# Eight of the 22 gate and up feature tiles of a ConvGLU formed from quarter blocks by seven products in place of eight

## The chip, the cores and the metric

The kernel runs on one core of a Trainium2 chip. The metric is the device time of one execution in microseconds (us). The median of three runs of the kernel before is 916.2 us, the lowest 915.85 and the highest 916.44 us. One further execution was recorded by the hardware profiler: it took 916.33 us, of which 914.6 us are the span from the first to the last instruction of the program, so 1.7 us lie around the span.

## The reference

One encoder layer over 512 tokens of width 1024, all in float32: a layer norm, a mixer of two attention head groups, a cross-attention to 256 memory tokens, and a gated feed-forward block, each followed by a residual sum and a layer norm. The change concerns the last block only. Cut to it, with 2816 features:

```python
def conv_glu(h, w_gate, w_up, conv_w, conv_b, w_down):
    g = h @ w_gate                      # (512, 1024) @ (1024, 2816)
    g = conv of width 3 along the tokens, per feature, plus conv_b
    return (gelu(g) * (h @ w_up)) @ w_down
```

## The kernel before, in words

**Arithmetic.** [...] To keep accuracy, every operand is split into a rounded part `hi` and the rest `lo`, and each product is made of three matmuls: hi·hi, hi·lo and lo·hi. The split takes one copy on ScalarE (ACT, line 134) and one subtraction on VectorE (DVE, line 136); the function is `split`, line 132.

**The gate and up stage.** The normed activations `h` lie transposed on chip in `h2T`, a pair (hi, lo), 8 blocks of 128 model rows by 512 tokens. `to_T` (line 202) makes them for 128 tokens at a time: eight transposes on TensorE into PSUM, then the split out of PSUM (lines 211 and 212). The 2816 features are 22 tiles of 128 (`NF`). For each tile f, `w_cols` (line 142) loads 1024 x 128 of `w_gate` and of `w_up` over SyncE's (SP's) DMA queue into a `raw` buffer and splits it. `gemm_fm` (line 168) then runs 8 x 3 matmuls with the weight block stationary and 512 tokens moving, once for gate (PSUM tag `g`) and once for up (PSUM tag `s`). The tail of the tile (lines 1356 to 1365) makes the convolution with one activation on ACT (Identity with scale and bias) and two scalar_tensor_tensor on DVE that read the gate sum in PSUM, then Gelu on ACT, then the product with up on DVE, written to `act[:, f, :]`.

**The first two tiles.** While the last 256 tokens are not yet normed and transposed, the gate and up of tiles 0 and 1 are begun on the first 256 tokens: `pre_gemm(i, 0)` runs 24 matmuls with 256 moving columns, and `pre_gemm(i, 1)` runs the other 256 columns later (lines 1328 to 1343). They use the PSUM tags `t`, `o` and both buffers of `g`.

**The stage behind.** The down product (from line 1394) takes the 22 tiles of `act` one after the other: it splits each into buffers of the tag `x`, splits 128 rows of `w_down`, and runs 24 matmuls of 512 columns for each.

**What sets the order.** Each engine runs its own queue in order. Within `manual_schedule` the order of TensorE is the order of the program text; everywhere else, and for ACT and DVE throughout the feed-forward block, a planner orders the instructions when the program is built. The loop over f in the kernel before is outside such a block, so there the planner orders TensorE too. Buffers are rotated by tags, and an instruction that takes a buffer waits until its last reader is done: `raw` has 3 buffers, `hi` and `lo` have 6 each (three feature tiles ahead), `gb` 2, `c` 3 (the convolution), `x` 12. PSUM has two buffers of `g` (one bank each), two of `s` (two banks each), one `t` and one `o`.

Of the kernel before, what the change touches and what calls it, by code (L numbers as in the profile page):

```python
# [9 lines left out]
F32 = mybir.dt.float32  # L10
F32R = mybir.dt.float32r
I32 = mybir.dt.int32
AF = mybir.ActivationFunctionType
ALU = mybir.AluOpType
# [3 lines left out]
P = 128  # L18
D = 1024
S = 512  # L20
NB = S // P
KD = D // P
# [3 lines left out]
NF = DFF // P  # L26
# [22 lines left out]
]  # L49

MEM_AT = (2, 0)
WARM = (12, 3)
CI, CF, CS, CMA, CM1, CM3 = 0, 128, 129, 130, 514, 770
CW = 898
# [17 lines left out]
def hymba_layer(ctx: ExitStack, tc: tile.TileContext, A, cst_d, out):  # L72
    nc = tc.nc
    X = mybir.AxisListType.X

    def pool(name, bufs=1, side="left", space=None):
        kw = {} if space is None else {"space": space}
        if space is None:
            kw["side"] = side
        return tc.tile_pool(name=name, bufs=bufs, **kw)  # L80

    cpool = ctx.enter_context(pool("const", side="right"))
    wpool = ctx.enter_context(pool("weights", side="right"))
    spool = ctx.enter_context(pool("small", bufs=3, side="right"))
    xpool = ctx.enter_context(pool("x2k", side="right"))
    spool.tile([P, 32], F32, tag="sfill", bufs=1, name="sfill")
    dpool = ctx.enter_context(tc.tile_pool(name="scratch", bufs=1, space=DRAM))

    cst = cpool.tile([P, CW], F32, name="cst")
    ident = cst[:, CI : CI + P]  # L90
    mhalf = cpool.tile([P, 1], F32, name="mhalf")
# [47 lines left out]
    def wsplit(raw, shape, eng=None):  # L139
        return split(raw, shape, wpool, "hi", 6, wpool, "lo", 6, eng)  # L140

    def w_cols(w, c0, eng=None):
        raw = wpool.tile([P, KD, P], F32, tag="raw", bufs=3, name="raw")
        nc.sync.dma_start(raw, w.rearrange("(k p) f -> p k f", p=P)[:, :, c0 : c0 + P])
        return wsplit(raw, [P, KD, P], eng)
# [10 lines left out]
    def on_pe(ins):  # L156
        if pe["pin"]:
            pe["pin"] = False
            tc.keep_in_program_order(ins)

    def pin():

        pe["pin"] = True

    def mm(o, l, r, first, last):
        on_pe(nc.tensor.matmul(o, l, r, start=first, stop=last))  # L166

    def gemm_fm(ps, wt, T, c0, n):
        whi, wlo = wt
        thi, tlo = T  # L170
        for k in range(KD):
            mm(ps, whi[:, k, :], thi[:, k, c0 : c0 + n], k == 0, False)
            mm(ps, whi[:, k, :], tlo[:, k, c0 : c0 + n], False, False)
            mm(ps, wlo[:, k, :], thi[:, k, c0 : c0 + n], False, k == KD - 1)
# [18 lines left out]
    def ps_tile(tag, bufs, shape=None):  # L193
        return gpool.tile(shape or [P, 512], F32, tag=tag, bufs=bufs, name=tag)

    def g_tile():
        return ps_tile("g", 2)

    def s_tile():
        return ps_tile("s", 2, [P, 2, 512])  # L200

    def to_T(t, T, b):
        ps = s_tile()
        for i in range(KD):
            f = i % 4 * P
            on_pe(nc.tensor.transpose(ps[:, i // 4, f : f + P], t[:, i * P : (i + 1) * P], ident))  # L206
        for i in range(2):
            k = slice(4 * i, 4 * i + 4)
            src = ps[:, i, :].rearrange("p (k t) -> p k t", k=4)
            hi = T[0][:, k, b * P : (b + 1) * P]  # L210
            nc.scalar.copy(hi, src)
            nc.vector.tensor_tensor(T[1][:, k, b * P : (b + 1) * P], src, hi.bitcast(F32), ALU.subtract)

    mid = ExitStack()
    tpool = mid.enter_context(pool("tT"))
# [18 lines left out]
    h = [(oA, oB)[b // 2][:, 2 * (b % 2) : 2 * (b % 2) + 2, :].rearrange("p a f -> p (a f)") for b in range(NB)]  # L234
# [134 lines left out]
    with tc.manual_schedule(engines={nc.tensor.engine, nc.vector.engine, nc.scalar.engine}):  # L369
# [5 lines left out]
        def busy(n, ps=None):  # L375
            for _ in range(n):
                mm((spare if ps is None else ps)[:, 0:P], ones_t, ones_t, True, True)

        busy(WARM[0])
        gps = [g_tile(), g_tile()]  # L380
# [3 lines left out]
        for n in range(2):  # L384
            mm(bt[n], ones_t, rows[:, 1, n, :], True, True)
        busy(WARM[1])
        vps = [g_tile(), g_tile()]
        two = s_tile()
# [106 lines left out]
        hl(3, *all_k)  # L495
        spill(2)

        rc = cpool.tile([P, S], F32, name="rc")
        rsn = cpool.tile([P, S], F32, name="rsn")
        posi = zs[:, 0, :].bitcast(I32)  # L500
        nc.sync.dma_start(posi, A["positions"].partition_broadcast(P)[:, 0, :])
        ang = zs[:, 2, :]
# [429 lines left out]
    with tc.manual_schedule(engines={nc.tensor.engine}):  # L932
# [125 lines left out]
        for c in range(KD):  # L1058
            whi, wlo = w_cols(w_xk, c * P)
            done("B2")  # L1060
            ps = g_tile()
# [52 lines left out]
        for hf in range(2):  # L1114
            wts = load_win(hf * 512)
            for b in range(NB):
                ps = g_tile()
# [6 lines left out]
    h = [hp[b] for b in range(NB)]  # L1124
# [28 lines left out]
    def U_pair():  # L1153
        return (
            U.tile([P, KD, S], F32R, tag="Uhi", name="Uhi"),
            U.tile([P, KD, S], F32R, tag="Ulo", name="Ulo"),
        )
# [80 lines left out]
    pin()  # L1238
    with tc.manual_schedule(engines={nc.tensor.engine}):
        to_T(h[0], h1T, 0)  # L1240
        for hf in range(2):
            dil_add(3, hf, dil_mm(3, hf))
        layer_norm(h[3], g1, b1)
        to_T(h[1], h1T, 1)
        proj_xv(1, [ps_tile("t", 1), ps_tile("o", 1)])
        kv(0)
        to_T(h[2], h1T, 2)
        wq = [w_cols(w_xq, c * P) for c in range(4)]
        part = [g_tile(), g_tile(), ps_tile("t", 1)]
# [50 lines left out]
        h2T = U_pair()  # L1300
# [16 lines left out]
    fp = ctx.enter_context(pool("ffn"))  # L1317
# [2 lines left out]
    nc.scalar.dma_start(cw[66:88, :], A["conv_b"][0].rearrange("(c p) -> c p", p=P))  # L1320
    cwT = fp.tile([P, 128], F32, name="cwT")[:, 0:88]
    act = fp.tile([P, NF, S], F32, name="act")
    pre = {}
    pin()
    with tc.manual_schedule(engines={nc.tensor.engine}):
        pre = [[None, ps_tile("t", 1)], [None, ps_tile("o", 1)], [None, g_tile()], [None, g_tile()]]

        def pre_gemm(i, s2):
            if s2 == 0:
                pre[i][0] = w_cols(A[("w_gate", "w_up")[i % 2]][0], i // 2 * P)  # L1330
            gemm_fm(pre[i][1][:, s2 * 256 : (s2 + 1) * 256], pre[i][0], h2T, s2 * 256, 256)

        to_T(h[2], h2T, 2)
        pre_gemm(0, 0)
        pre_gemm(1, 0)
        tp = s_tile()[:, 0, 0:88]
        nc.tensor.transpose(tp, cw, ident[0:88, 0:88])
        nc.vector.tensor_copy(cwT, tp)
        pre_gemm(2, 0)
        to_T(h[3], h2T, 3)  # L1340
        pre_gemm(3, 0)
        for i in range(4):
            pre_gemm(i, 1)

    pin()
    for f in range(NF):
        if f < 2:
            pg, pu = pre[2 * f][1], pre[2 * f + 1][1]
        else:
            wg = w_cols(A["w_gate"][0], f * P)  # L1350
            wu = w_cols(A["w_up"][0], f * P)
            pg = g_tile()
            pu = s_tile()[:, 0, :]
            gemm_fm(pg, wg, h2T, 0, S)
            gemm_fm(pu, wu, h2T, 0, S)
        c = fp.tile([P, S], F32, tag="c", bufs=3, name="c")
        nc.scalar.activation(c, pg, AF.Identity, scale=cwT[:, 22 + f : 23 + f], bias=cwT[:, 66 + f : 67 + f])
        nc.vector.scalar_tensor_tensor(
            c[:, 1:S], pg[:, 0 : S - 1], cwT[:, f : f + 1], c[:, 1:S], ALU.mult, ALU.add
        )  # L1360
        nc.vector.scalar_tensor_tensor(
            c[:, 0 : S - 1], pg[:, 1:S], cwT[:, 44 + f : 45 + f], c[:, 0 : S - 1], ALU.mult, ALU.add
        )
        nc.scalar.activation(c, c, AF.Gelu)
        nc.vector.tensor_tensor(act[:, f, :], c, pu, ALU.mult)
    g3, b3 = (wpool.tile([P, D], F32, tag="gb", bufs=2, name="gb3") for _ in range(2))
    nc.sync.dma_start(g3, A["ln3_g"][0].partition_broadcast(P))
    nc.sync.dma_start(b3, A["ln3_b"][0].partition_broadcast(P))
    with gs:
        acc = [[ps_tile("t", 1), ps_tile("o", 1)]]  # L1370
        for b in range(1, NB):
            two = s_tile() if b != 2 else None
# [16 lines left out]
        def down_ops(k):  # L1389
            w = w_rows(A["w_down"][0], k, 1, 0, D)  # L1390
            a = split(act[:, k, :], [P, S], xpool, "x", 12, xpool, "x", 12)
            return w, a

        for k in range(KO):
            w, a = down_ops(k)
# [48 lines left out]
```

## Time and profile before

| what | value |
|---|---|
| profiled execution | 916.33 us (median of the runs 916.2) |
| its span | 914.6 us |
| TensorE (PE) busy | 903.1 us, 99% |
| weight loads (PEld) busy | 760.0 us, 83% |
| VectorE (DVE) busy | 497.2 us, 54% |
| ScalarE (ACT) busy | 362.3 us, 40% |
| GpSimd (POOL) busy | 127.5 us, 14% |
| mean granted TensorE clock | 0.998 |

The profile names each group of instructions by its line, its engine and the program's tile names (written tile, arrow, read tiles). A matmul's own duration overlaps with its neighbours', so the cost of one matmul in a stream is the distance between starts, not its duration. The chain of work that ended last follows, from the last instruction back, what released each step; a stretch of it that names only TensorE is a stretch where nothing but TensorE's own rate set the time. The gate and up stage runs from about 545 us to 787 us, the down product from there to the end.

### The profile page before, as it was taken

What the parts mean: (1) busy time and instruction counts of PE and PEld (TensorE: products, weight loads), DVE (VectorE), ACT (ScalarE), POOL (GpSimd) and SP (SyncE); (2) the same over time, 40 slices, a digit from 0 to 9 for tenths busy, and PEclk for the clock granted to TensorE, in tenths of its full rate; (3) what the DMA queues carried; (4) which work ended last, traced back from release to release, by engine and by line L of the source; (5) the groups of instructions that cost most, each with busy time, mean ns of one, the idle gap of its engine ahead of it and who ended that gap; (6) DMA issues with size and microseconds to landing.
All of it is one profiled execution on the core that took longest, in us unless ns stands there. A gap on an engine that the chain in (4) does not pass through costs nothing.

```text
span 914.6 us, 12181 instructions
## 1 busy us (share of the span) xinstructions
PE 903.1 (99%) x4809; PEld 760.0 (83%) x4809; DVE 497.2 (54%) x856; ACT 362.3 (40%) x636; POOL 127.5 (14%) x106
## 2 busy tenths in 40 slices
PE   9999999999999999999999999999999999999996
PEld 7778987898878898789988889888888888888885
DVE  7975146435446677778565595543344434333346
ACT  4564436415545476314553224432332333222210
POOL 1064034332444420010000010000000000000001
PEclk9999999999999999999999999999999999999999
DMA  6762041314222338316212314333333332223201
GB/s 218 227 209 72 22 138 48 87 52 116 70 70 58 98 105 249 116 47 184 77 64 68 108 44 150 116 99 108 93 92 92 101 107 92 92 93 98 86 24 70
DMA packets 116940, 92.81 MB, mean 101 GB/s; under 512 B 12472, under 2 KB 100752, under 8 KB 116882
## 3 DMA queue, kind: packets, MB, share of 16 engines
q1 hardware_dynamic: 116048, 89.80, 32.3%
q10 hardware_dynamic: 834, 2.22, 0.6%
q8 instruction: 38, 0.62, 0.3%
q14 instruction: 20, 0.16, 0.1%
HBM read 87.82 MB, written 4.19 MB: 101 GB/s over the span
## 4 chain that ended last, share of the span: by engine, by line
PE 95%; DVE 3%; DMA 1%; issue 0%; ACT 0%; POOL 0%; DVEq 0%; ACTq 0%
PE g L166 53%; PE s L166 27%; PE t L166 4%; PE o L166 4%; PE o L690 3%; PE s L678 2%; PE s L206 1%; DMA vt<-in_ln_in_g_dram 1%; PE s L1221 0%; DVE lo L277 0%; DVE oA L343 0%; DVE st L307 0%; DVE Tlo L362 0%; POOL zs L526 0%; DVE mx L1202 0%
## 5 line engine op out<-in xcount | busy, mean ns | idle before, releaser
L136 DVE TENSOR_TENSOR lo<-raw,hi 128x1024 fp32r<-128x1024 f32 x142 | 176.7, 1246 | 156.9 <-ACT hi L134 154.6
L134 ACT CAST hi<-raw 128x1024 fp32r<-128x1024 f32 x142 | 149.2, 1052 | 221.1 <-PE g L166 163.3
L166 PE MATMUL g<-Thi,hi 128*128 128x512 f32 x240 | 94.8, 395 | 0.0
L166 PE MATMUL g<-Tlo,hi 128*128 128x512 f32 x240 | 94.3, 393 | 0.0
L166 PE MATMUL g<-Thi,lo 128*128 128x512 f32 x240 | 94.0, 392 | 0.0
L166 PE MATMUL g<-Uhi,hi 128*128 128x512 f32 (+1 forms) x256 | 93.2, 364 | 0.0
L166 PE MATMUL g<-Uhi,lo 128*128 128x512 f32 (+1 forms) x256 | 92.8, 363 | 0.0
L166 PE MATMUL g<-Ulo,hi 128*128 128x512 f32 (+1 forms) x256 | 92.8, 363 | 0.0
L107 POOL TENSOR_TENSOR rs<-ve,mhalf 128x1 f32<-128x1 f32 x18 | 15.4, 854 | 530.0 <-DVE ve L113 521.8
L526 POOL TENSOR_TENSOR zs<-zs,rsn 128x512 f32<-128x512 f32 x29 | 59.3, 2046 | 147.1 <-DVE zs L525 147.1
L166 PE MATMUL g<-hi,Thi 128*128 128x512 f32 x184 | 71.6, 399 | 0.0
L166 PE MATMUL g<-hi,Tlo 128*128 128x512 f32 x184 | 71.0, 395 | 0.5 <-DVE Tlo L1169 0.5
L166 PE MATMUL g<-lo,Thi 128*128 128x512 f32 x184 | 70.6, 395 | 0.4 <-DVE lo L277 0.4
L166 PE MATMUL s<-Uhi,lo 128*128 128x512 f32 x160 | 62.3, 389 | 0.0
L166 PE MATMUL s<-Ulo,hi 128*128 128x512 f32 x160 | 62.3, 389 | 0.0
L166 PE MATMUL s<-Uhi,hi 128*128 128x512 f32 x160 | 62.2, 389 | 0.0
L524 DVE TENSOR_TENSOR zs<-g,rc 128x512 f32<-128x512 f32 x29 | 20.0, 688 | 68.1 <-PE g L166 31.5
L166 PEld LDWEIGHTS g<-Uhi,lo 128*128 128x128 f32 x256 | 48.3, 189 | 7.6
L166 PEld LDWEIGHTS g<-Uhi,hi 128*128 128x128 f32 x256 | 48.3, 189 | 7.4
L166 PEld LDWEIGHTS g<-Ulo,hi 128*128 128x128 f32 x256 | 48.2, 188 | 7.4
L166 PEld LDWEIGHTS g<-Thi,hi 128*128 128x128 f32 x240 | 45.1, 188 | 11.0 <-issue 0.9
L166 PEld LDWEIGHTS g<-Tlo,hi 128*128 128x128 f32 x240 | 45.1, 188 | 10.3 <-issue 1.4
(330 smaller groups left out, 1765.3 us busy)
## 6 DMA issues: line engine op xcount, KB each, us to landing
raw<-in_w_in_dram SPq DMA_DIRECT2D x37, 512.0 KB, 3.8
raw<-in_w_gate_dram SPq DMA_DIRECT2D x22, 512.0 KB, 3.8
raw<-in_w_up_dram SPq DMA_DIRECT2D x22, 512.0 KB, 3.9
raw<-in_w_down_dram SPq DMA_DIRECT2D x22, 512.0 KB, 3.3
raw<-in_w_xk_dram SPq DMA_DIRECT2D x8, 512.0 KB, 3.9
raw<-in_w_xv_dram SPq DMA_DIRECT2D x8, 512.0 KB, 3.3
raw<-in_w_xq_dram SPq DMA_DIRECT2D x8, 512.0 KB, 4.8
raw<-in_w_xo_dram SPq DMA_DIRECT2D x8, 512.0 KB, 3.3
```

The costliest lines, as they stand in the source:

```text
L107: nc.gpsimd.tensor_tensor(out_, in_, mhalf, ALU.pow)
L134: nc.scalar.copy(hi, raw)
L136: (eng or nc.vector).tensor_tensor(lo, raw, hi.bitcast(F32), ALU.subtract)
L166: on_pe(nc.tensor.matmul(o, l, r, start=first, stop=last))
L206: on_pe(nc.tensor.transpose(ps[:, i // 4, f : f + P], t[:, i * P : (i + 1) * P], ident))
L524: nc.vector.tensor_tensor(zc, ps, rc, ALU.mult)
L526: nc.gpsimd.tensor_tensor(sh, sh, rsn, ALU.mult)
L678: nc.tensor.transpose(tp[:, k, :], s_, ident)
L690: nc.tensor.matmul(o[HJ[j], t0:t1], lhs(j), rhs(j), start=i == 0, stop=i == len(parts) - 1)
```

## The change

Eight feature tiles (5, 7, 9, ..., 19) no longer run `gemm_fm` for gate and up. The gate and up weights of a tile are stacked as a 2 x 2 arrangement of quarter blocks (gate or up by upper or lower half of the 1024 model rows), and the activations as 2 x 2 (upper or lower half of the rows by first or last 256 tokens). The 2 x 2 product of blocks is then made by seven block products in place of eight, with sums and differences of blocks ahead of and behind them (the Winograd form of Strassen's scheme). A block product is `product`: 4 row blocks x 3 matmuls with 256 moving columns.

What is added around the products:

- `to_T` for the last 256 tokens also copies the unrounded transposed values on ACT into `raw_u`, which lies in the part of `act` for tiles 14 to 21 that is still unused.
- `t_forms`, called after tiles 2, 3 and 4, makes four combinations of the activation quarters on DVE, in three portions, each split into hi and lo. They live in the 12 buffers of `x` for the first three and in `t4` and the two buffers of a new tag `rope` for the fourth. Their scratch `r`, `q` shares the 3 buffers of tag `c`. The rope tables `rc`, `rsn`, which are used only early in the kernel, now have the tag `rope` and are allocated first in their pool.
- For each of the eight tiles, four combinations of weight quarters on DVE (`s1` to `s4`), and splits of 28 row blocks (in place of 16).
- For each of the eight tiles, one ACT copy and four DVE sums that put gate and up together in an SBUF tile `gu`, from which the unchanged tail (now the function `ffn_tail`) reads.

The loop over f now stands in a `manual_schedule` block for TensorE. The tail of a tile is otherwise the same. The reads of `w_gate` and `w_up` are as many and as large as before.

```diff
+SEVEN = (5, 7, 9, 11, 13, 15, 17, 19)
...
+    rope = [cpool.tile([P, S], F32, tag="rope", bufs=2, name=n) for n in ("rc", "rsn")]
...
-    def to_T(t, T, b):
+    def to_T(t, T, b, raw=None):
...
+        for i in range(2 if raw is not None else 0):
+            k = slice(4 * i, 4 * i + 4)
+            nc.scalar.copy(raw[:, k, b * P : (b + 1) * P], ps[:, i, :].rearrange("p (k t) -> p k t", k=4))
...
+    raw_u = act[:, NF - KD : NF, :]
...
-        to_T(h[2], h2T, 2)
+        to_T(h[2], h2T, 2, raw_u)
...
-        to_T(h[3], h2T, 3)
+        to_T(h[3], h2T, 3, raw_u)
...
+    HT, HK = S // 2, KD // 2
+    sl, sr = slice(0, HT), slice(HT, S)
+    B11, B12, B21, B22 = (
+        [t[:, HK * i : HK * (i + 1), n] for t in h2T] for i in range(2) for n in (sl, sr)
+    )
+    R12, R22 = (raw_u[:, HK * i : HK * (i + 1), sr] for i in range(2))
+    T = {}
+    t4 = fp.tile([P, HK, HT], F32R, name="t4")
...
+    def t_parts(n, i, r):
+        if n < 3:
+            hl = [xpool.tile([P, 2, HT], F32R, tag="x", bufs=12, name="x") for _ in range(2)]
+        else:
+            hl = [two_k(t4, i), cpool.tile([P, 2, HT], F32R, tag="rope", bufs=2, name="t4l")]
+        nc.scalar.copy(hl[0], r)
+        nc.vector.tensor_tensor(hl[1], r, hl[0].bitcast(F32), ALU.subtract)
+        T.setdefault(n, []).append(hl)
+
+    def t_tile():
+        return fp.tile([P, 2, HT], F32, tag="c", bufs=3, name="r")
+
+    def t_forms(j):
+        if j == 2:
+            for i in range(2):
+                r = t_tile()
+                nc.vector.tensor_tensor(r, two_k(R22, i), two_k(R12, i), ALU.subtract)
+                t_parts(2, i, r)
+            return
+        r, q = t_tile(), t_tile()
+        for t, B in ((r, B11), (q, B21)):
+            nc.vector.tensor_tensor(t, two_k(B[0], j).bitcast(F32), two_k(B[1], j).bitcast(F32), ALU.add)
+        nc.vector.tensor_tensor(r, two_k(R12, j), r, ALU.subtract)
+        t_parts(0, j, r)
+        nc.vector.tensor_tensor(r, two_k(R22, j), r, ALU.subtract)
+        t_parts(1, j, r)
+        nc.vector.tensor_tensor(q, q, r, ALU.subtract)
+        t_parts(3, j, q)
...
+    def product(ps, wt, u):
+        for k in range(HK):
+            for a, b in ((0, 0), (0, 1), (1, 0)):
+                mm(ps, wt[a][:, k, :], u(b, k), k + a + b == 0, k == HK - 1 and a == 1)
...
+    def seven(f):
...
+        s13, s24 = (wpool.tile([P, KD, P], F32, tag="gb", bufs=2, name="gb") for _ in range(2))
+        s1, s3, s2, s4 = (t[:, HK * i : HK * (i + 1), :] for t in (s13, s24) for i in range(2))
+        A11, A12 = parts(raw[0], KD)
+        nc.vector.tensor_tensor(s1, a21, a22, ALU.add)
+        nc.vector.tensor_tensor(s3, a11, a21, ALU.subtract)
+        S1, S3 = parts(s13, KD)
+        nc.vector.tensor_tensor(s2, s1, a11, ALU.subtract)
+        nc.vector.tensor_tensor(s4, a12, s2, ALU.subtract)
+        S2, S4 = parts(s24, KD)
+        (A22,) = parts(a22, HK)
+        p1_ = ps_tile(("t", "o")[f % 2], 1)[:, sl]
+        product(p1_, A11, quarter(B11))
+        two = [g_tile(), g_tile(), s_tile()[:, 0, :]]
+        product(two[0][:, sl], A12, quarter(B21))
+        product(two[1][:, sl], S1, moving(0))
+        product(two[1][:, sr], S3, moving(2))
+        product(two[0][:, sr], S2, moving(1))
+        product(two[2][:, sl], S4, quarter(B22))
+        product(two[2][:, sr], A22, moving(3))
+        gu = fp.tile([P, 2 * S], F32, tag="gu", bufs=1, name="gu")
+        u34 = act[:, f, :]
...
+        nc.scalar.copy(gu[:, S + HT :], p1_)
+        nc.vector.tensor_tensor(pair(gu[:, 0:S]), pair(two[0]), twice(gu[:, S + HT :]), ALU.add)
+        nc.vector.tensor_tensor(pair(u34), pair(two[1]), twice(gu[:, sr]), ALU.add)
+        nc.vector.tensor_tensor(gu[:, S + HT :], two[1][:, sl], u34[:, sr], ALU.add)
+        nc.vector.tensor_tensor(gu[:, HT : S + HT], two[2], u34, ALU.add)
+        ffn_tail(f, gu[:, 0:S], gu[:, S:])
...
+    with tc.manual_schedule(engines={nc.tensor.engine}):
+        for f in range(2):
+            ffn_tail(f, pre[2 * f][1], pre[2 * f + 1][1])
+        for f in range(2, NF):
+            if f in SEVEN:
+                seven(f)
+                continue
...
+            gemm_fm(pg, wg, h2T, 0, S)
+            gemm_fm(pu, wu, h2T, 0, S)
+            ffn_tail(f, pg, pu)
+            if f < 5:
+                t_forms(f - 2)
```

`parts` is the split of a raw tile into `hi` and `lo` buffers, `quarter` and `moving` pick the moving block from `h2T` or from a combination, `two_k` takes two of four row blocks.

More of the change, by code (lines that the diff above doesn't have):

```diff
@@ L496, in hymba_layer @@
         spill(2)
-        rc = cpool.tile([P, S], F32, name="rc")
-        rsn = cpool.tile([P, S], F32, name="rsn")
+        rc, rsn = rope
         posi = zs[:, 0, :].bitcast(I32)
@@ L1343, in hymba_layer, with ffn_tail @@
             pre_gemm(i, 1)
[L1345 to L1355, printed above, removed]
+    def ffn_tail(f, pg, pu):
         c = fp.tile([P, S], F32, tag="c", bufs=3, name="c")
@@ L1365, in hymba_layer, with two_k @@
         nc.vector.tensor_tensor(act[:, f, :], c, pu, ALU.mult)
+    HT, HK = S // 2, KD // 2
[6 more added lines that the diff above has]
+    t4 = fp.tile([P, HK, HT], F32R, name="t4")
+    def two_k(v, i):
+        return v[:, 2 * i : 2 * i + 2]
+    def t_parts(n, i, r):
[6 more added lines that the diff above has]
+        T.setdefault(n, []).append(hl)
@@ new lines, in moving, with quarter, parts @@
+    def moving(n):
+        return lambda w, k: T[n][k // 2][w][:, k % 2, :]
+    def quarter(q):
+        return lambda w, k: q[w][:, k, :]
+    def product(ps, wt, u):
+        for k in range(HK):
+            for a, b in ((0, 0), (0, 1), (1, 0)):
+                mm(ps, wt[a][:, k, :], u(b, k), k + a + b == 0, k == HK - 1 and a == 1)
+    def parts(raw, n):
+        hi = wpool.tile([P, n, P], F32R, tag="hi", bufs=6, name="hi")
+        nc.scalar.copy(hi, raw)
+        lo = wpool.tile([P, n, P], F32R, tag="lo", bufs=6, name="lo")
+        nc.vector.tensor_tensor(lo, raw, hi.bitcast(F32), ALU.subtract)
+        return [[t[:, HK * i : HK * (i + 1), :] for t in (hi, lo)] for i in range(n // HK)]
@@ new lines, in seven, with twice, pair @@
+    def seven(f):
+        raw = []
+        for name in ("w_gate", "w_up"):
+            raw.append(wpool.tile([P, KD, P], F32, tag="raw", bufs=3, name="raw"))
+            nc.sync.dma_start(raw[-1], A[name][0].rearrange("(k p) f -> p k f", p=P)[:, :, f * P : (f + 1) * P])
+        a11, a12, a21, a22 = (t[:, HK * i : HK * (i + 1), :] for t in raw for i in range(2))
+        s13, s24 = (wpool.tile([P, KD, P], F32, tag="gb", bufs=2, name="gb") for _ in range(2))
[19 more added lines that the diff above has]
+        u34 = act[:, f, :]
+        def twice(v):
+            return v.unsqueeze(1).to_broadcast([P, 2, HT])
+        def pair(v):
+            return v.rearrange("p (a t) -> p a t", a=2)
+        nc.scalar.copy(gu[:, S + HT :], p1_)
[4 more added lines that the diff above has]
+        ffn_tail(f, gu[:, 0:S], gu[:, S:])
@@ new lines, in hymba_layer @@
+    pin()
+    with tc.manual_schedule(engines={nc.tensor.engine}):
[5 more added lines that the diff above has]
+                continue
+            wg = w_cols(A["w_gate"][0], f * P)
+            wu = w_cols(A["w_up"][0], f * P)
+            pg = g_tile()
+            pu = s_tile()[:, 0, :]
+            gemm_fm(pg, wg, h2T, 0, S)
[3 more added lines that the diff above has]
+                t_forms(f - 2)
```

## The prediction
> **What bounds the kernel now.** I read the page's busy times and the chain of the whole program first, then the chain in order of time over the stage that changes, then its groups and windows.
>
> ```profile
> span 914.6 us, 12181 instructions
> PE 903.1 (99%) x4809; PEld 760.0 (83%) x4809; DVE 497.2 (54%) x856; ACT 362.3 (40%) x636; POOL 127.5 (14%) x106
> PE 95%; DVE 3%; DMA 1%; issue 0%; ACT 0%; POOL 0%; DVEq 0%; ACTq 0%
> ```
>
> TensorE carries 95% of the chain. In the stage itself the chain has nothing else; start, length, what, and the number of matmuls:
>
> ```profile
> 544.34 0.87 PE s L206 x8
> 545.21 2.87 PE t L166 x24
> 548.08 2.88 PE o L166 x24
> ...
> 562.88 2.88 PE o L166 x24
> 565.76 5.76 PE g L166 x48
> ...
> 602.37 5.44 PE g L166 x24
> 607.81 5.44 PE s L166 x24
> ...
> 781.89 5.44 PE s L166 x24
> 787.33 0.68 PE t L166 x3
> ```
>
> A gemm of 24 matmuls with 512 moving columns takes 5.44 us, so 226.7 ns each. The rows at 545, 548 and 562 are the first and second halves of tiles 0 and 1: 24 matmuls with 256 columns in 2.88 us, 120 ns each. That is a little more than half of 226.7: by the two values a matmul has 106.7 ns per 256 columns and a fixed 13.3 ns. These are the matmuls that the change uses, with the same three products per row block, already measured in this kernel. Windows (us, then busy us and number for PE, weight loads, DVE, ACT, POOL, then clock and DMA):
>
> ```profile
> 680.00:691.00 11.00, 11.00 (x50) 9.13 (x49) 4.67 (x6) 3.42 (x4) 0.00 (x0) 1.00 0.32 95
> 558.00:603.00 45.00, 45.00 (x246) 39.20 (x245) 23.39 (x28) 20.19 (x25) 0.00 (x0) 1.00 0.36 107
> ```
>
> In the steady stage DVE is busy 4.67 of 11.00 us; the clock is full. So time is to be had only by less TensorE work, as long as DVE and ACT stay under it.
>
> **Part 1, the products.** Before, a tile costs 2 x 5.44 = 10.88 us. After, one of the eight costs 7 products x 12 matmuls = 84 matmuls with 256 columns, 84 x 0.120 = 10.08 us. The columns fall by an eighth (84 x 256 against 48 x 512), which is 12 units of 256 columns, 12 x 0.1067 = 1.28 us, but 36 more matmuls pay the fixed 13.3 ns each, 0.48 us; what is left is 0.80 us per tile, 6.4 us for eight. With 2.87 in place of 2.88 it is 6.7 us. A product changes its bank and its moving tile every 12 matmuls; the chain goes from `t` to `o` to `g` in those rows without a gap, so I put that at 0.
>
> [...]
>
> **Part 2, DVE and ACT in the steady stage.** The groups of the window from 620 to 790 us, and single forms from the whole run (busy, mean ns, idle before):
>
> ```profile
> L136 DVE TENSOR_TENSOR lo<-raw,hi 128x1024 fp32r<-128x1024 f32 x32 | 39.2, 1225 | 68.5 <-ACT hi L134 66.8
> L134 ACT CAST hi<-raw 128x1024 fp32r<-128x1024 f32 x31 | 32.7, 1055 | 81.1 <-PE g L166 65.8 <-PE s L166 15.3
> L1357 ACT ACTIVATE c<-g,cwT 128x512 f32<-128x512 f32 x16 | 12.4, 777 | 0.0
> L1364 ACT ACTIVATE c<-c 128x512 f32<-128x512 f32 x16 | 10.1, 632 | 33.9 <-DVE c L1361 33.9
> ...
> L136 DVE TENSOR_TENSOR lo<-act,hi 128x512 fp32r<-128x512 f32 x22 | 15.2, 690 | 53.4 <-ACT hi L134 53.4
> L134 ACT CAST hi<-act 128x512 fp32r<-128x512 f32 x22 | 13.7, 622 | 63.4 <-PE s L166 62.4 <-DVE act L1365 1.0
> L905 DVE TENSOR_TENSOR x<-s,x 128x256 fp32r<-128x256 f32 x8 | 3.4, 419 | 1.8 <-ACT x L904 1.8
> L1067 ACT COPY kmT<-g 128x256 f32<-128x256 f32 x8 | 2.9, 367 | 0.0
> ```
>
> One of the eight tiles adds on DVE: splits of 12 more row blocks, 1.5 x 1.23 = 1.84 us; four weight sums of 512 elements at 0.69, 2.76 us; three sums of 512 and one of 256 behind the products, 3 x 0.69 + 0.42 = 2.49 us. With the 4.67 of a plain tile that is 11.8 us, more than the tile's own 10.08 us on TensorE. But a plain tile always follows: 11.8 + 4.7 = 16.5 of 10.08 + 10.88 = 20.96 us, 79%. ACT gets 1.5 x 1.06 + 0.37 = 1.95 us on 2 x 1.06 + 0.78 + 0.63 = 3.52, so 9.0 us per pair, 43%. Neither is the bound on average; what hides them is that the splits run ahead. The `hi` rows show how far: in the steady stage a split waits for "PE g" or "PE s", the release of its buffer, never for data, so the weights lie ready as early as the six buffers allow. A pair takes six (4 + 2), so weights are still made about one pair ahead: the splits of the next such tile can start as its predecessor's products 2, 4, 6 and 7 end, and have some 18 us each (product 2 ends 2.88 us into a pair of 20.96). `raw` is let go by those same splits, so the loads (the same number on SP's queue) stay ahead too. I put the wait for weights at 0; without that cover it would be a tile's 3.5 splits and four sums on DVE, 3.5 x 1.23 + 2.76 = 7.1 us.
>
> The one short cover is the PSUM buffer `g`. The plain tile after takes the bank of products 2 and 5, which is free when DVE has added `p1_` to it. Product 5 ends 2 x 12 x 0.120 = 2.88 us before that tile starts. One split may run ahead on DVE (1.23), then the sum (0.69): 1.9 us, so 0 in the likeliest case with 1 us to spare. The two gaps bound it: 0 and, with three more DVE operations ahead, 1.65 us per tile (rival C).
>
> **Part 3, the start of the loop.** Before, the planner slipped tile 2's up matmuls in between the second halves of tiles 0 and 1:
>
> ```profile
> 557.98 0.28 PE L166 MATMUL t<-Uhi,hi 128*128 128x256 f32 x1
> 558.10 0.40 PE L166 MATMUL s<-Uhi,hi 128*128 128x512 f32 x1
> ```
>
> After, TensorE keeps the text's order: four half gemms (11.5 us, 557.98 to 569.5), then tile 2's gate, which needs the first buffer of `g`, that of tile 1's gate. DVE and ACT around its release before:
>
> ```profile
> 568.62 1.04 ACT L134 CAST hi<-raw 128x1024 fp32r<-128x1024 f32 x1
> 569.57 0.77 ACT L1357 ACTIVATE c<-g,cwT 128x512 f32<-128x512 f32 x1
> ...
> 570.84 0.74 DVE L1358 SCALAR_TENSOR_TENSOR c<-g,cwT,c 128x511 f32<-128x511 f32 x1
> 571.50 0.68 DVE L136 TENSOR_TENSOR lo<-act,hi 128x512 fp32r<-128x512 f32 x1
> 572.10 0.74 DVE L1361 SCALAR_TENSOR_TENSOR c<-g,cwT,c 128x511 f32<-128x511 f32 x1
> ```
>
> That gate gemm ended at 565.76 + 2.88 = 568.64 and its bank was free at 572.84, 4.2 us later. After, it ends at 566.6, so the bank is free at 570.8, or 570.2 without the `act` split in between: TensorE waits 0.7 to 1.3 us, once. I take 1.0; the ends are 0 and, with one or two operations of `t_forms` ahead, 2.5.
>
> **Part 4, the combinations of activations.** The rows from DVE and ACT for it:
>
> ```profile
> 563.92 1.23 DVE L136 TENSOR_TENSOR lo<-raw,hi 128x1024 fp32r<-128x1024 f32 x1 [5.96 <-ACT hi L134]
> ...
> 595.13 0.69 DVE L136 TENSOR_TENSOR lo<-act,hi 128x512 fp32r<-128x512 f32 x1 [0.69 <-ACT hi L134]
> ...
> L211 ACT CAST Uhi<-s 128x512 fp32r<-128x512 f32 x16 | 9.3, 585 | 48.6 <-PE s L206 46.6 <-DVE Ulo L212 1.9
> ```
>
> The portions are 20 DVE operations of 512 elements (13.8 us) and 8 ACT copies (5.0 us), which must be there about 3 to 9 us into tile 5, which starts near 570.5 + 3 x 10.88 = 603. DVE was busy 23.39 us from 558 to 603. Four `act` splits (2.8 us, the first at 571.50, the fourth at 595.13) leave, since the `x` buffers now hold combinations until tile 19; 13.8 and tile 5's extra 4.6 come: 39.0 of 45 us, 87%. It fits, barely; I put 0, with ends 0 and 4. The four raw copies on ACT near 548 and 556 are 4 x 0.59 = 2.4 us and sit behind the Uhi copies that TensorE waits for; 0. The early `act` splits move to tiles 20 and 21, under 2 x 10.88 us of matmuls; without that cover they would cost a split, 1.3 us, once.
>
> **Sum.** Against the profiled execution: 916.33 - 6.4 + 1.0 = 910.9 us. The median of the runs shown is 0.13 lower, which changes nothing.
>
> **Rivals.** A measurement of this kernel tells about 0.2%, 1.8 us, from no change.
>
> A, the forecast: TensorE runs without gaps but one. 910.9, own range 909.6 (2.87 us and no wait) to 912.5. Chance 0.62.
>
> B, the combinations are late for tile 5, once. For it: 87%, and the third portion's four DVE operations and two ACT copies (4.0 us) come behind tile 4 in the text; against: nothing in them needs tile 4, and DVE idled there, 5.96 us in one piece before 563.92. 3.5 us more: 914.4. Chance 0.14.
>
> C, slower: in every one of the eight tiles the sum that frees `g` stands on DVE behind the next weights' work. Two splits and two sums (2 x 1.23 + 2 x 0.69 = 3.84) and the sum itself make 4.5 us against 2.88 of cover: 1.65 us, eight times, 13.2 us: 924.1. It decides from 0.68 us per tile on, where 8 x 0.68 takes the 5.4 us. For it: DVE's queue is in order (before, a split did run ahead of the convolution, as above at 568.62 and 569.57 on ACT) and it carries 79%; against: those splits are released at other moments than product 5's end. Chance 0.08.
>
> D, the same wait but shorter, 0.3 to 0.9 us per tile, middle 0.6: 4.8 us, 915.7. Chance 0.11.
>
> E, a matmul costs by its columns alone: 8 x 1.36 = 10.9, 906.4 with the wait at the start. The rows with 2.88 speak against. Chance 0.02.
>
> F, slower: short matmuls are held up by their weight loads. The window below, with 256 columns, has a weight load under way at all times, where the window from 680 us had 9.13 of 11.00.
>
> ```profile
> 545.20:553.60 8.40, 8.40 (x73) 8.40 (x72) 7.89 (x14) 2.12 (x3) 0.92 (x1) 1.00 0.82 233
> ```
>
> At 128 columns the eight transposes at 544.34 take 0.87/8 = 109 ns each, twice their columns' share, so a floor near 109 ns is there; 120 lies above it. Were the products held at 150 ns, a tile would take 12.6 us and the whole 931; the change loses from 10.88/84 = 129.5 ns on. [...] Chance 0.03.
>
> **How the numbers follow.** Faster by over 0.2%: A, E and most of B, 0.77. Within: most of D and the rest of B, 0.12. Slower: C and F, 0.11. The range 909.4 to 915.5 takes in A with its ends, B and the nearer part of D, and leaves out C, E, F and the rest of D.
>
> **What would show it.** Right: in the chain, for each of the eight tiles 12 matmuls on `o` in 1.44 us, 48 on `g` in 5.76 and 24 on `s` in 2.88; DVE near 79% from 603 to 780 us; one idle stretch of TensorE of about 1 us before tile 2, ended by the second L1361-type operation. B would show as one wait of TensorE in tile 5 for an `x` tile; C and D as eight waits at the start of tiles 6, 8, ..., 20 for the sum on DVE; F as longer runs of matmuls without a wait. Above 130 ns per matmul, or waits of more than 0.7 us per tile, would make the prediction wrong.

## The result and the profile after

The changed kernel takes 911.52 us (median of 6 runs, 910.43 to 911.75); the kernel before, in runs beside it, 916.32 us. The ratio is 0.9946, with a 95% interval of 0.9933 to 0.9959: 4.8 us faster. 910.9 was predicted. The profiled execution took 911.27 us, with a span of 909.5 us.

The page of the changed kernel, and its chain in order of time from the second halves of tiles 0 and 1 on (start, length, what, matmuls):

```profile
span 909.5 us, 12905 instructions
PE 896.6 (99%) x5097; PEld 768.3 (84%) x5097; DVE 560.2 (62%) x956; ACT 385.0 (42%) x672; POOL 127.2 (14%) x106
PE 95%; DVE 3%; ACT 1%; DMA 1%; issue 0%; POOL 0%; DVEq 0%; ACTq 0%
```

```profile
558.13 2.88 PE t L168 x24
...
563.89 5.66 PE g L168 x47
...
569.57 1.05 ACT hi L136
...
570.63 5.72 PE g L168 x24
...
603.55 1.43 PE o L168 x12
604.99 5.76 PE g L168 x48
610.75 2.88 PE s L168 x24
613.63 5.47 PE g L168 x24
...
624.53 1.43 PE o L168 x12
...
782.27 0.68 PE t L168 x3
```

TensorE still carries 95%, and there is one break in the stage, ahead of tile 2. All waits of TensorE in the stage (in total, times, longest):

```profile
PE g L168 <- ACT hi L136: 1.0, 1, 1.0
```

Three numbers tell where the 5.06 us between the two profiled executions come from. Tile 5 starts at 603.55, where it started at 602.37 before: 1.18 us later. From tile 5 to the down product it takes 782.27 - 603.55 = 178.72 us in place of 787.33 - 602.37 = 184.96: 6.24 us less, 0.78 for each of the eight tiles. A pair of tiles repeats every 20.98 us (603.55 to 624.53). From the down product to the end of the span both take 127.2 us.

The windows of one pair and of the stretch ahead of it (us, then busy us and number for PE, weight loads, DVE, ACT, POOL; then the clock, the busy share of the DMA engines and GB/s):

```profile
603.55:624.53 20.98, 20.98 (x135) 19.09 (x134) 15.47 (x20) 9.53 (x13) 0.00 (x0) 1.00 0.35 101
558.00:603.00 45.00, 44.01 (x241) 38.26 (x240) 34.46 (x47) 21.06 (x29) 0.00 (x0) 1.00 0.27 80
```

TensorE has no gap in a pair, and DVE is busy 15.47 of 20.98 us, 74%. DVE's queue around the end of tile 5's products shows the short cover that the prediction named:

```profile
610.31 1.23 DVE L1421 TENSOR_TENSOR lo<-gb,hi 128x1024 fp32r<-128x1024 f32 x1 [0.86 <-ACT hi L1419]
611.45 0.68 DVE L1459 TENSOR_TENSOR gu<-g,gu 128x512 f32<-128x512 f32 x1
```

Product 5 ends at 610.75. One split runs ahead, then L1459 frees the bank at 612.13, and the plain tile needs it at 613.63: 1.5 us to spare.

### The profile page after: what moved, and what is told of

Read it like the earlier page. It is cut to its first block, busy times and chain, and to the rows that moved or that the text cites. A ratio compares the mean times of both kernels' runs of the same rounds, so it can differ in the third digit from the quotient of the medians.

```text
span 909.5 us, 12905 instructions
## 1 busy us (share of the span) xinstructions
PE 896.6 (99%) x5097; PEld 768.3 (84%) x5097; DVE 560.2 (62%) x956; ACT 385.0 (42%) x672; POOL 127.2 (14%) x106
## 4 chain that ended last, share of the span: by engine, by line
PE 95%; DVE 3%; ACT 1%; DMA 1%; issue 0%; POOL 0%; DVEq 0%; ACTq 0%
PE g L168 54%; PE s L168 24%; PE o L168 5%; PE t L168 4%; PE o L694 3%; PE s L682 2%; PE s L208 1%; DMA vt<-in_ln_in_g_dram 1%; PE s L1225 0%; DVE lo L282 0%; DVE oA L348 0%; DVE st L312 0%; DVE Tlo L367 0%; POOL zs L530 0%; DVE mx L1206 0%
## 5 line engine op out<-in xcount | busy, mean ns | idle before, releaser
L138 DVE TENSOR_TENSOR lo<-raw,hi 128x1024 fp32r<-128x1024 f32 x126 | 157.2, 1249 | 86.6 <-ACT hi L136 85.9
L136 ACT CAST hi<-raw 128x1024 fp32r<-128x1024 f32 x126 | 132.3, 1051 | 141.5 <-PE g L168 92.5
L168 PE MATMUL g<-Uhi,hi 128*128 128x512 f32 (+1 forms) x224 | 77.5, 346 | 1.0 <-ACT hi L136 1.0
L168 PE MATMUL g<-Ulo,hi 128*128 128x512 f32 (+1 forms) x224 | 77.1, 344 | 0.0
L168 PE MATMUL g<-Uhi,lo 128*128 128x512 f32 (+1 forms) x224 | 77.0, 344 | 0.0
L168 PE MATMUL g<-x,hi 128*128 128x256 f32 x320 | 58.8, 284 | 0.0
L168 PEld LDWEIGHTS g<-Thi,hi 128*128 128x128 f32 x240 | 45.1, 188 | 11.1 <-issue 0.9
L168 PEld LDWEIGHTS g<-Thi,lo 128*128 128x128 f32 x240 | 45.1, 188 | 9.3
L168 PEld LDWEIGHTS g<-x,hi 128*128 128x128 f32 x320 | 50.0, 192 | 0.5 <-issue 0.3
L168 PEld LDWEIGHTS g<-hi,Tlo 128*128 128x128 f32 x184 | 42.2, 230 | 6.4 <-DVE Tlo L1173 1.0
L138 DVE TENSOR_TENSOR lo<-act,hi 128x512 fp32r<-128x512 f32 x22 | 14.8, 690 | 52.8 <-ACT hi L136 52.8
```

What stands on the lines that cost most here:

```text
L136: nc.scalar.copy(hi, raw)
L138: (eng or nc.vector).tensor_tensor(lo, raw, hi.bitcast(F32), ALU.subtract)
```

## The experiments

Each is compared with the kernel before on its own chip (medians there 915.9 to 916.4 us). The theory: a tile by seven products saves 0.78 us on TensorE, the fixed order of TensorE loses about 1.2 us once ahead of tile 2, and the rest of the new work lies beside the matmuls as long as nothing that frees a buffer for TensorE stands too late in DVE's queue. Rivals: the gain or loss comes from elsewhere in the change; DVE's load counts in itself.

**1. No tile by seven products.** The combinations are still made, though nothing reads them.

```diff
-SEVEN = (5, 7, 9, 11, 13, 15, 17, 19)
+SEVEN = ()
```

> All 22 tiles are plain gemms again; the combinations of activations, the raw copies, the new place of the rope tables and the text's order of TensorE in the loop stay. My theory (the gain is eight times 0.78 us from the products, minus about 1.2 us lost once where tile 2's gate waits for its PSUM bank under the fixed order): 916.3 + 1.2 = 917.5 us, 1.2 above before, with one idle stretch of TensorE of about 1 us ahead of tile 2. Rival 1 (the rest of the change, its order or its addresses, also brings or takes time): anything else, and at 911.5 the products would bring nothing. Rival 2 (the combinations cost time as well): more than 918.5.

Measured: 917.41 us, ratio 1.0011 (1.0001 to 1.0020), about 1.0 us above before. The products bring the whole gain, and the combinations' 20 DVE operations cost nothing visible. The chain of this run has the same single break:

```profile
569.93 1.05 ACT hi L136
...
570.99 5.72 PE g L168 x24
```

**2. Tile 2's up ahead of its gate.**

```diff
-            gemm_fm(pg, wg, h2T, 0, S)
-            gemm_fm(pu, wu, h2T, 0, S)
+            for ps, w in ((pu, wu), (pg, wg)) if f == 2 else ((pg, wg), (pu, wu)):
+                gemm_fm(ps, w, h2T, 0, S)
```

> The changed kernel, but in tile 2 alone the up gemm runs ahead of the gate gemm. The up sum takes a bank of the tag s, which is free. My theory (the wait ahead of tile 2 is for tile 1's gate bank in the tag g, a matter of order alone): the wait of 1.09 us goes, and nothing else changes: 911.5 - 1.1 = 910.4 us. Rival (the wait is for something that both gemms need, such as an ACT split that the profile names as releaser): the wait stays, 911.5 us.

Measured: 909.73 us, ratio 0.9926 (0.9910 to 0.9941). Its chain:

```profile
557.59 2.88 PE t L168 x24
...
569.11 5.47 PE s L168 x24
574.58 10.88 PE g L168 x48
...
601.78 1.43 PE o L168 x12
```

The break is gone. From the start of the second halves to tile 5 it is 601.78 - 557.59 = 44.19 us, against 603.55 - 558.13 = 45.42 in the changed kernel: 1.23 us. The other half microsecond of the 1.8 between the medians is there already at 557.59, ahead of the edit, and is not its doing. So the wait was a matter of order. In the changed kernel the profile puts it down to an ACT split that ends at 570.61. DVE's convolution, which reads tile 1's gate bank, ended at 570.49:

```profile
569.74 0.75 DVE L1356 SCALAR_TENSOR_TENSOR c<-g,cwT,c 128x511 f32<-128x511 f32 x1
```

The two ends are 0.12 us apart, and the experiment alone shows only that the up gemm needs neither. The trace separates them. That split makes tile 4's up weights: it is the last of four behind 558 us, and the loads in SP's queue place these at tiles 3 and 4. Nor did the gate gemm wait for it: its first weight load starts at 570.60, before the split's end, and its first matmul 0.14 us after the convolution's end. In run 4, TensorE starts the same 0.14 us after the sum that frees the bank there. So it waited for the bank of `g`.

**3. The same eight tiles by eight products of 256 columns.** Gate and up as two halves of 256 tokens, 96 matmuls.

```diff
-            if f in SEVEN:
-                seven(f)
-                continue
...
-            gemm_fm(pg, wg, h2T, 0, S)
-            gemm_fm(pu, wu, h2T, 0, S)
+            for ps, w in ((pg, wg), (pu, wu)):
+                n = S // 2 if f in SEVEN else S
+                for c0 in range(0, S, n):
+                    gemm_fm(ps[:, c0 : c0 + n], w, h2T, c0, n)
```

> The eight tiles are made by the plain eight products, but in matmuls of 256 columns: gate and up each as two halves of 256 tokens, 96 matmuls in place of 84 of the changed kernel and of 48 of before. The combinations are made and not read. My theory (a matmul costs 106.7 ns per 256 columns and a fixed 13.3 ns): a tile takes 96 x 0.120 = 11.52 us, 0.64 us more than a plain tile, eight times 5.1 us: the time of the run with no such tiles plus 5.1, near 917.5 + 5.1 = 922.6 us. Rival E (columns alone cost): no difference to that run, 917.5 us. Rival F (the short matmuls are held up by weight loads in this stage, and the gain comes in spite of it): above 925 us.

Measured: 922.41 us, ratio 1.0064 (1.0047 to 1.0082): 5.0 us above run 1, 0.63 us per tile for 48 extra matmuls, 13.0 ns each. That is the fixed part, and rivals E (no fixed part) and F (short matmuls held up by their weight loads) both fall.

**4. The sum that frees the bank, four times.**

```diff
-        nc.vector.tensor_tensor(pair(gu[:, 0:S]), pair(two[0]), twice(gu[:, S + HT :]), ALU.add)
+        for _ in range(4):
+            nc.vector.tensor_tensor(pair(gu[:, 0:S]), pair(two[0]), twice(gu[:, S + HT :]), ALU.add)
```

> The changed kernel, but the DVE sum that frees the PSUM bank for the next plain tile is made four times over (same operands, same result), 1.9 us more DVE work in each of the eight tiles; in DVE's queue two splits of the next weights now stand between the repeats, one of them for a buffer that only product 7 frees. My theory (DVE's average is no bound at 74%, but this sum has about 1.5 us to spare, and DVE's queue is in order): the bank comes free near 16.2 us after the tile's start at 603.6 rather than at 612.1, some 2.5 us after the plain tile could start: eight times 2.5, 20 us, about 931 us. If only the repeats counted and no split stood between them it would be eight times 0.4, 3 us. Rival (DVE is fully hidden below 100%, and the place of an operation does not matter): 911.5 us.

Measured: 940.59 us, ratio 1.0261 (1.0239 to 1.0283), 29 us above the changed kernel. DVE's queue in tile 5 (L1460 is the sum here), and TensorE's waits for it:

```profile
610.14 1.41 DVE L1460 TENSOR_TENSOR gu<-g,gu 128x512 f32<-128x512 f32 x2
611.88 1.23 DVE L1421 TENSOR_TENSOR lo<-gb,hi 128x1024 fp32r<-128x1024 f32 x1 [0.33 <-ACT hi L1419]
613.02 0.68 DVE L1460 TENSOR_TENSOR gu<-g,gu 128x512 f32<-128x512 f32 x1
613.62 0.68 DVE L1421 TENSOR_TENSOR lo<-raw,hi 128x512 fp32r<-128x512 f32 x1
614.22 0.68 DVE L1460 TENSOR_TENSOR gu<-g,gu 128x512 f32<-128x512 f32 x1
```

```profile
PE g L168 <- DVE gu L1460: 19.1, 7, 2.7
```

The splits stand between the repeats, as the queue's order said, and the plain tile waits 2.7 us. The waits are the size that was expected (19.1 us). What comes on top is mostly a second effect. The profiled execution took 942.19 us, 30.9 above the changed kernel's. 19.1 us are these seven waits, and 1.7 us are one wait for a split that the down product needs. 11.1 us come from the eight gate gemms behind the waits, which run longer than 5.47 us. Against that, tile 5 started 1.3 us earlier here. Two of those gemms:

```profile
615.05 7.31 PE g L168 x24
640.60 8.58 PE g L168 x24
```

Behind five of the seven waits for the sum the gate gemm took 7.2 us or more, behind the other two 5.7. In the five the granted clock (last column but two) fell to 0.50. Here is one wait with a drop behind it, then one without:

```profile
612.60:616.01 3.41, 0.96 (x4) 0.86 (x5) 3.34 (x7) 0.25 (x1) 0.00 (x0) 1.00 0.05 13
616.01:619.42 3.41, 3.41 (x9) 2.64 (x8) 2.18 (x4) 0.97 (x2) 0.00 (x0) 0.50 0.48 141
...
691.11:694.52 3.41, 1.61 (x7) 1.38 (x8) 3.34 (x6) 0.00 (x0) 0.00 (x0) 1.00 0.29 82
694.52:697.93 3.41, 3.41 (x17) 2.82 (x16) 1.73 (x4) 1.45 (x2) 0.00 (x0) 1.00 0.24 72
```

Seven equal waits gave five drops, so the length of the wait alone does not decide. The drops start at 616.01, 639.91, 667.21, 742.3 and 766.2 us, whole multiples of 3.41 us apart, and last 3.41 us, the second one 6.83. What brings them about is not shown; no run tests it by itself. In the changed kernel the wait of 1.0 us left the clock at 1.00 and cost 0.28 us more (a gemm of 5.72 us in place of 5.44).

**5. The same extra work on DVE, ahead of the products.**

```diff
-        nc.vector.tensor_tensor(s4, a12, s2, ALU.subtract)
+        for _ in range(4):
+            nc.vector.tensor_tensor(s4, a12, s2, ALU.subtract)
```

> The changed kernel, but the fourth weight sum is made four times over: the same three extra DVE operations of 512 elements per tile as in the run with the later sum, 1.8 us, but ahead of the products instead of behind them. DVE goes from 15.5 to 17.3 us of a pair's 20.98 (74% to 82%). My theory (average load below the pair's time costs nothing, place does): no wait of TensorE added, 911.5 us. Rival (DVE's load itself costs, as the 29 us of the run with the later sum might be read): some 3 us per 0.3 us of wait, 914 us or more.

Measured: 911.26 us, ratio 0.9948 (0.9936 to 0.9961), the changed kernel's time. The window of one pair:

```profile
624.00:645.00 21.00, 21.00 (x134) 19.09 (x133) 17.10 (x23) 8.94 (x12) 0.00 (x0) 1.00 0.35 101
```

Runs 4 and 5 each add three DVE operations of the same size per tile. In one place they cost 29 us, in the other nothing, with DVE at 81% (17.10 of 21.00 us). Place decides, not load, up to there.

**6. All 17 tiles from 5 on by seven products.**

```diff
-SEVEN = (5, 7, 9, 11, 13, 15, 17, 19)
+SEVEN = tuple(range(5, 22))
```

> All 17 tiles from 5 to 21 by seven products. DVE needs for such a tile 15.5 - 4.7 = 10.8 us against 10.07 us on TensorE, and no plain tile comes between to catch up. My theory (DVE becomes the bound): 17 tiles at 10.8 us or more against 10.88 before, so at best 917.5 - 1.4 = 916 us, and more with in-order waits: 916 to 930 us, with waits of TensorE for DVE in most of these tiles. Rival (DVE is hidden, the gain grows with the number of tiles): 917.5 - 17 x 0.78 = 904.2 us.

Measured: 944.95 us, ratio 1.0306 (1.0288 to 1.0324). The rival is out, but the theory's reason was wrong too, and the number outside its range. The waits, a window, and DVE's queue in one of the tiles:

```profile
PE g L168 <- DVE gu L1459: 11.9, 7, 1.9
PE g L168 <- DVE gu L1461: 11.2, 13, 1.6
```

```profile
640.00:660.00 20.00, 18.29 (x130) 17.95 (x131) 15.73 (x24) 7.61 (x10) 0.00 (x0) 0.85 0.18 53
```

```profile
665.01 0.69 DVE L1460 TENSOR_TENSOR act<-g,gu 128x512 f32<-128x512 f32 x1
666.62 0.69 DVE L1433 TENSOR_TENSOR gb<-raw 128x512 f32<-128x512 f32 x1 [0.92 <-DMA raw<-in_w_up_dram]
667.23 0.68 DVE L1434 TENSOR_TENSOR gb<-raw 128x512 f32<-128x512 f32 x1
667.83 0.42 DVE L1461 TENSOR_TENSOR gu<-g,act 128x256 f32<-128x256 f32 x1
```

DVE isn't full: 15.73 of 20.00 us in this window, and 81% from 620 to 760 us. L1461, which frees the second bank of `g`, was ready at 665.70, but two weight sums of the next tile stand ahead of it, and the first waits 0.92 us for a weight load. That is place again: an operation that waits for a DMA, in a queue that is worked in order, ahead of one that TensorE waits for. The waits for L1459, the sum that frees the first bank, come behind weight splits that DVE works first.

The clock adds its part, 0.85 in the window above, though no wait here is longer than 1.9 us:

```profile
635.85:639.26 3.41, 1.53 (x13) 1.35 (x12) 2.72 (x4) 0.37 (x1) 0.00 (x0) 1.00 0.53 154
639.26:642.67 3.41, 2.16 (x11) 1.89 (x10) 3.27 (x5) 1.86 (x2) 0.00 (x0) 0.50 0.00 0
```

TensorE was busy 1.53 us, 45% of the 3.41 us ahead of this drop. In run 4, worked out from the starts of the gemms and the waits of 2.7 us ahead of them, it was busy 26 to 44% ahead of the five drops, and the two stretches of 45 and 47% in which its other two waits end had none behind them.

**7. The same, with the weight sums on GpSimd.**

```diff
-        nc.vector.tensor_tensor(s1, a21, a22, ALU.add)
+        nc.gpsimd.tensor_tensor(s1, a21, a22, ALU.add)
...
```

> All 17 tiles by seven products, and the four weight sums of each on GpSimd in place of DVE. By the rope's GpSimd operation on 128x512 (2.05 us each) they take 8.2 us of a tile's 10.07; DVE falls to 10.8 - 2.4 = 8.4 us (83%). My theory (the load on DVE, not the products or the buffers, is what stops the scheme from being used on every tile): 917.5 - 17 x 0.78 = 904.2, plus up to 1 us at the start of the down product, whose act splits now wait for the last tile: 904 to 906 us. Rival 1 (GpSimd's sums come too late or slow DVE): 910 us or more, with waits for them. Rival 2 (the PSUM banks do not allow two such tiles in a row): waits at each tile, the time of the run with 17 tiles on DVE alone.

Measured: 913.59 us, ratio 0.9972 (0.9963 to 0.9981). Much better than run 6, so the banks do allow such tiles in a row, but 9 us short of the theory: what its first rival said. A window, and groups of DVE from 625 to 765 us:

```profile
640.00:660.00 20.00, 18.79 (x154) 18.38 (x154) 19.82 (x20) 8.57 (x12) 12.13 (x8) 1.00 0.28 83
```

```profile
L1421 DVE TENSOR_TENSOR lo<-raw,hi 128x1024 fp32r<-128x1024 f32 x13 | 24.8, 1908 | 0.0
L1353 DVE SCALAR_TENSOR_TENSOR c<-gu,cwT,c 128x511 f32<-128x511 f32 x13 | 17.9, 1379 | 0.0
...
L1356 DVE SCALAR_TENSOR_TENSOR c<-gu,cwT,c 128x511 f32<-128x511 f32 x13 | 9.8, 751 | 0.5
L1459 DVE TENSOR_TENSOR gu<-g,gu 128x512 f32<-128x512 f32 x13 | 8.9, 681 | 0.0
```

Now DVE is full, 19.82 of 20.00 us, although it has less to do. Several of its operations with both inputs in SBUF have grown: the split of 1024 elements from 1225 to 1908 ns, the first operation of the convolution (L1353) from 744 to 1379 (both against run 6). Those that read PSUM have not: L1459 takes 681 ns (683 in run 6), and 0.68 us also at 621.94, while a GpSimd sum runs from 621.43 to 623.17. Nor has the convolution's second operation (L1356, 751 ns against 744). The single operations show when it happens; two of DVE, then GpSimd's sum at that time:

```profile
682.12 1.78 DVE L1353 SCALAR_TENSOR_TENSOR c<-gu,cwT,c 128x511 f32<-128x511 f32 x1
683.93 0.75 DVE L1356 SCALAR_TENSOR_TENSOR c<-gu,cwT,c 128x511 f32<-128x511 f32 x1
```

```profile
681.19 2.16 POOL L1437 TENSOR_TENSOR gb<-raw,gb 128x512 f32<-128x512 f32 x1
```

L1353 runs into the sum and takes 1.78 us; L1356 starts when the sum is over and takes 0.75. So it goes for all 13 of each from 625 to 765 us: the eight L1353 that meet a GpSimd sum take 1.78 us, the five that meet none 0.74, and no L1356 meets one. What couples the two engines is not shown. TensorE waited 7.4 us in 11 places for L1459, most of the 9 us.

**8. The same, with tile 2's up ahead of its gate** (the edits of 2, 6 and 7).

> The run before this, and tile 2's up ahead of its gate. The two effects are at different places and add: 1.2 us (the wait ahead of tile 2) less than that run, 903 us. Rival (with less slack in the first tiles the combinations of activations come late for tile 5, and the gain is eaten by a wait there): no difference.

Measured: 912.66 us, ratio 0.9965 (0.9953 to 0.9978), 0.9 us less than run 7 with overlapping intervals. The break ahead of tile 2 is gone from its chain and no wait came in its place at tile 5, but the difference in time is no more than the runs' scatter.

**9. Two of three tiles.** With tile 2's up first, as in 2.

```diff
-SEVEN = (5, 7, 9, 11, 13, 15, 17, 19)
+SEVEN = (5, 6, 8, 9, 11, 12, 14, 15, 17, 18, 20, 21)
```

> Two tiles by seven products, then a plain one: 12 of the tiles from 5 to 21 (5, 6, 8, 9, ..., 20, 21), weight sums on DVE, and tile 2's up ahead of its gate. DVE needs 2 x 10.8 + 4.7 = 26.3 us of 2 x 10.07 + 10.88 = 31.0 us, 85%. My theory (DVE is the only limit, and 85% leaves enough to catch up in the plain tile): four tiles more than the run with up ahead, 909.7 - 4 x 0.78 = 906.6 us. Rival (what stops the scheme is two such tiles in a row, by the bank and the order on DVE, as in the run with 17 on DVE alone): waits of 1 us or more in each second tile and a lowered clock behind them, 912 us or more.

Measured: 911.90 us, ratio 0.9950 (0.9936 to 0.9963). Neither answer was right. The waits of TensorE, and the window of three tiles:

```profile
PE g L168 <- DVE gu L1459: 2.9, 5, 0.8
PE g L168 <- DVE x L1382: 0.6, 1, 0.6
```

```profile
651.00:682.00 31.00, 30.64 (x212) 28.52 (x212) 25.43 (x35) 14.59 (x18) 0.00 (x0) 1.00 0.33 95
```

The waits are 3.5 us, and the five gate gemms behind those for L1459 take 5.74 to 5.76 us in place of 5.47, 1.4 us together; that is 4.9 of the 5.3 us that are missing from the theory. DVE was at 25.43 of 31.00 us, 82%, close to run 5's 81% that cost nothing, and the sum that frees the bank stood behind splits and weight sums there, so place explains the waits and load need not; no run separates the two here. The combinations came 0.6 us late in tile 5 (the wait for `x`).

**10. Nine tiles, every second one up to 21.** With tile 2's up first.

> Tile 21 is made by seven products too (nine tiles, every second one), and tile 2's up runs ahead of its gate. My theory (each such tile with a plain one ahead gives 0.78 us; the combinations' buffers then go to the down product's act splits only in tile 21, with 5.8 us and less to go): 909.7 - 0.8 = 908.9 us. Rival (the late act splits hold up the start of the down product): a wait of 1 to 3 us there, 910 to 912 us.

Measured: 909.30 us, ratio 0.9927 (0.9915 to 0.9940), no wait of TensorE in the stage. Against run 2 (0.9926) the ratio has not moved: the expected 0.8 us is too little to be told from their intervals. The traces do show it in the stage. The down product starts here at the first, in run 2 at the second of these rows:

```profile
780.05 0.69 PE t L168 x3
```

```profile
780.50 0.68 PE t L168 x3
```

From tile 5 on that is 780.05 - 602.14 = 177.91 us, against 780.50 - 601.78 = 178.72 in run 2: 0.81 us less. From there to the end both take about 127.2 us, so nothing is lost at the start of the down product; tile 5 itself started 0.36 us later here. Runs 2 and 10 are the fastest versions tried.

## Why the prediction was right

- **The price of a matmul** (512 columns 226.7 ns, 256 columns 120, so 0.80 us per tile). Right: 0.78 in the changed kernel, and run 3 measured the fixed part by itself, 13.0 ns against 13.3. The 109 ns that rival F reads as a floor at 128 columns is no general one: in the profile before, 32 such matmuls of line 690, with weights of 128 x 64, took 1.97 us from 225.72 on, at most 62 ns each. The products of a tile took 1.43 + 5.76 + 2.88 = 10.07 us, and the first plain gemm after such a tile 0.03 us more than the others, 5.47 in place of 5.44.
- **The wait at the start** (1.0 us, once, by the text's order). Right in place, cause and size: TensorE waited 1.0 us for the bank. That the loss also came out near 1.0 holds some luck. The restart, 0.28 us, was left out; but before, the same stretch took 602.37 - 557.98 = 44.39 us, 0.20 more than run 2's 44.19, so against before only 1.03 us were lost in it. The other 0.15 of the 1.18 us by which tile 5 came later were there before the second halves of tiles 0 and 1 (558.13 for 557.98).
- **Weights ahead in time** (no wait). Right in the changed kernel: no wait for them in the stage.
- **DVE in the steady stage** (79%). It was 74%. The durations of single operations were added, and operations in a row start about 0.08 us before the end of the one ahead (0.60 us apart at 0.68, as in run 4's queue from 613.02 on), so the term was too large; nothing hung on it.
- **The combinations** (87% of DVE from 558 to 603, cost 0). DVE was at 34.46 of 45.00, 77%, and there was no wait in tile 5. Of the 4.5 us too much, about 1.5 are the same overlap; the rest is two splits and a product of the tail that ran only after 603 us. Rival B did not happen.
- **The bank of `g`** (2.88 us of cover, one split and the sum within it). Right, 1.5 us to spare where 1 was put. Run 4 brings about rival C's loss: the mechanism is real, and rival C, which left the clock at full speed, had no term for the longer gemms behind the waits.
- **The sum.** 916.33 - 6.24 + 1.18 = 911.27 us, the profiled time; predicted was 916.33 - 6.4 + 1.0. What remained wrong came later, in the expectations for more such tiles: there I took DVE's load for the limit. Run 6 shows place in its queue with DVE at 81%, run 7 a DVE made full (19.82 of 20.00 us) by operations that grew beside GpSimd's, and in run 9 place explains the waits at 82%, where load was not ruled out.

## What to carry to other kernels

An exchange of fewer, shorter matmuls for more vector work is priced by the measured distance between matmul starts at both lengths: here an eighth fewer columns became 7% of a tile, because the fixed 13 ns per matmul are paid more often. The extra vector work was free, up to a DVE 81% busy, as long as the operations that free a bank or buffer for TensorE were not queued behind work that waits for something later (in run 6, 0.92 us for a weight load); look at the order in that queue and at the one cover that is short, before adding up loads. Where a text's order is fixed for TensorE, look for a gemm that needs a bank just then, and put one ahead of it that does not (1.23 us in run 2).

## What the runs showed of the hardware

- Behind five of seven waits of TensorE of 2.7 us (run 4) the granted clock fell to 0.50 for 3.41 or 6.83 us, and a gemm of 5.47 us took up to 8.58. In run 6 it fell behind waits of at most 1.9 us. After the single wait of 1.0 us the clock stayed at 1.00 and the gemm took 5.72.
- In run 4 the five drops begin whole multiples of 3.41 us apart (at 616.01, 639.91, 667.21, 742.3 and 766.2), and TensorE was busy 26 to 44% of the 3.41 us ahead of each. Two stretches of 45 and 47% had no drop behind them there, and one of 45% in run 6 had one, so no sharp limit is shown.
- In run 7 the eight L1353 (DVE, inputs in SBUF) that met a GpSimd sum took 1.78 us, the five that met none 0.74. L1459, which reads PSUM, took 0.68 us on average, as in run 6, and also beside a sum.
